# Mixture-of-experts stage of a one-core encoder block: where the filler steps stand between the expert products, and how w1 and w3 lie in a weight block

## The chip, the cores and the metric

The kernel runs on one core of a Trainium2 chip. The metric is the device time of one launch in microseconds (us); less is better. The kernel before took 1903.09 us in the median of three runs (1902.76 to 1908.07).

## The reference, cut to what matters

The block takes 512 tokens of width 1024, mixes them along the sequence (a gated convolution and a state-space branch), and then sends every token through two of 64 experts. Only the second part is touched:

```python
# per expert e, on the tokens that were routed to it
hdn = jax.nn.silu(xblk @ w1[e]) * (xblk @ w3[e])   # w1, w3: 1024 x 512
y   = hdn @ w2[e]                                  # w2: 512 x 1024
h  += g2 * (weight of the token for e) * y         # scattered back to the tokens
```

All weights are float32: 2 MB (2,097,152 bytes) each for w1, w3 and w2 of an expert, 6.29 MB for an expert and 402.7 MB for all 64. Every expert has 64 slots for tokens; what is over that goes to a later round, which is not part of this story.

## The kernel before, in words

**Stages.** The first 800 us or so compute the modulation, the norms, the mixer and the routing. From then on the experts are worked off in 32 pairs (loop in line 1462), the two experts of a pair one behind the other. Four kinds of work run on TensorE (PE) there:

- **W**, in `hidden` (line 1289): the first product. For each of eight slices k of the width, two matmuls with the 64 tokens as stationary operand (64 columns of the array each, `128*64` in the profile) and 512 columns of weights moving: 256 of w1 and the same 256 of w3, one row of the operand `w[k // 4][:, k % 4, :, 256 * j:256 * j + 256]`. One matmul of the program stands as two records in the trace, so an expert has 32 records `ps_w<-wb,xg`.
- **Y**, in `second` (line 1311): the second product, 16 records `ps_y<-wb,ht`, also on 64 columns.
- **g**, a step of `gather` (line 1272): 12 bfloat16 matmuls of 128 columns, `ps_g<-S,hg`, with the full array, which collect 128 channels of the tokens of the next pair. Behind the fourth and the eighth step ScalarE copies four slices of `xg` out of PSUM.
- **c**, a step of `combine` (line 1337): two matmuls `ps_o<-yh,so` and `ps_o<-yl,so` with the full array and 512 columns, which scatter scaled outputs of the last pair to a tile of tokens; VectorE then adds the sum in PSUM to `h` (`h<-h,ps_o`). There are two such sums in PSUM (`po`, line 1225), used in turn, so the third step of a row needs the addition of the first to be over.

`hidden_t` puts two transposes (`ps_ht`) between W and Y. A pair needs eight g and eight c.

**The order on PE** is written out by hand (everything runs in program order on every engine). The table `FILL` (line 1375) has ten places for each of the two experts, divided by commas, and the experts by a semicolon. Places 0 to 7 stand ahead of the matmuls of slice k = 0 to 7, place 8 between W and the transposes, place 9 between the transposes and Y. `FILL0` to `FILL2` are for pairs 0 to 2 and `FILL3` is for the last, so `FILL` holds for the 28 pairs from 3 to 30:

```python
FILL = [v.split(",") for v in ",,,,c,,c,g,gg,gc;c,,c,g,c,,c,,gg,gc".split(";")]
...
for k in range(KD):
    fill(k)
    for j in range(2):
        PE.matmul(ps[64 * j:64 * j + 64], lhsT=xg[:, k, 64 * e:64 * e + 64],
                  rhs=w[k // 4][:, k % 4, :, 256 * j:256 * j + 256], start=(k == 0), stop=(k == KD - 1))
```

**The weights** come through a ring of eight blocks of 16 KB on every partition (`load_upto`, line 741), filled by the queue of SyncE (SP). An expert takes three: slices 0 to 3 of w1 and w3, slices 4 to 7 of both, and w2. At the start of the expert whose first block is b the program has asked for all blocks up to b + 7; a DMA waits on SP until the block that lay in its place has been read for the last time. For the first two blocks of an expert there are two DMAs of 1 MB (line 754), one from w1 and one from w3:

```python
t = t.rearrange("p (k i f) -> p k i f", i=2, k=4)
for k, m in [(0, 2), (2, 2)] if fine else [(0, 4)]:
    for i, n_ in enumerate(("w1", "w3")):
        SP.dma_start(t[:, k:k + m, i], a[n_][e].rearrange("(p k) f -> p k f", k=KD)[:, 4 * part + k:4 * part + k + m])
```

In HBM the four slices of a partition are one piece of 8 KB. In the block the 2 KB rows of w1 and w3 alternate. w2 comes in one DMA of 2 MB (line 765), its pieces 8 KB on both sides. `fine` holds for the early blocks up to 23 and the last expert, whose DMAs are cut in two.

**Between the pairs** (`scale_y`, line 1321) VectorE scales Y, ScalarE rounds it to `yh`, VectorE takes the rest `yl`, GpSimd makes the 0/1 matrix `so`. These feed the c of the next pair.

Of the kernel before, what the change touches and what calls it, by code (L numbers as in the profile page):

```python
# [19 lines left out]
T = 512          # tokens  # L20
D = 1024         # model width
KD = D // P      # k-tiles of the model width; channel d = 8 * p + k
NE = 64          # experts
CAP = 64         # slots of an expert per round
# [39 lines left out]
# columns of the packed per-partition parameters  # L64
# [9 lines left out]
# order in which the 128-column tiles of w_in are used  # L74
# [21 lines left out]
class Meter:  # L96
    """An engine whose instructions' time is added up (us, from their shapes)."""
# [31 lines left out]
def hybrid_block(ctx: ExitStack, tc: tile.TileContext, a, out, dbg=None, stage=9):  # L129
# [11 lines left out]
    # ------------------------------------------------------------ constants  # L141
# [20 lines left out]
    def rstd_start(r, v):  # L162
        """r = 1/sqrt(v + eps) of a [P, 512] array (v may lie in PSUM)."""
        S.activation(r, v, AF.Ln, bias=epsc, scale=1.0)
        S.activation(r, r, AF.Exp, scale=-0.5)

    def rstd_end(r, t, v):
        """A Newton step for it."""
        V.tensor_mul(t, r, r)
        V.scalar_tensor_tensor(t, v, EPS, t, op0=OP.add, op1=OP.mult)  # L170
        V.tensor_scalar(t, t, -0.5, 1.5, op0=OP.mult, op1=OP.add)
        V.tensor_mul(r, r, t)

    def rsqrt_small(r, v, t1, t2, scale=1.0):
        """r = 1/sqrt(scale * v + eps) of a few columns, with a Newton step."""
        V.tensor_scalar(t1, v, scale, EPS, op0=OP.mult, op1=OP.add)
        S.activation(t2, t1, AF.Sqrt)
        V.reciprocal(r, t2)
        V.tensor_mul(t2, r, r)
        V.tensor_mul(t2, t2, t1)  # L180
        V.tensor_scalar(t2, t2, -0.5, 1.5, op0=OP.mult, op1=OP.add)
        V.tensor_mul(r, r, t2)

    # The mixer is emitted in the order in which its engines run it. It goes in slots: one tile of
    # weights each, of about five microseconds of the tensor engine; between the products of two
    # slots stand the small steps of the state-space branch and of the norms, and the vector engine
    # works on the long convolution in what the slots leave.
# [8 lines left out]
    accyf = blky.tile([P, KD * T], F32, name="accy")     # y_ssm, later h  # L196
# [4 lines left out]
    accv = blk.tile([P, KD, T], F32, name="accv")     # conv of the GLU branch  # L201
# [30 lines left out]
    def warm_up(n):  # L232
        """Keeps the tensor engine's clock up where it would wait for others."""
# [4 lines left out]
    # ------------------------------------------------------------ adaLN (shift, scale), norm1, first slots  # L238
    with tc.tile_pool(name="start", bufs=1, side="right") as sp:
# [25 lines left out]
        for k in range(KD):  # L265
            for sec, acc in ((0, acc_sh), (1, acc_sc)):
                w_ = ada_load(k, sec)
                ada_step(acc, w_, k)
                if WK <= k < WKE:                              # keeps the tensor engine's clock up
# [9 lines left out]
        # the sums over the partitions, channels on partitions; more than the one column, for the clock  # L279
# [29 lines left out]
    # ------------------------------------------------------------ buffers of the slots  # L309
# [4 lines left out]
    lsum = wkA.tile([P, T], F32, name="lsum")           # sum over the channels' tiles  # L314
# [3 lines left out]
    causal = wk.tile([P, P], F32, name="causal")       # [s, l]: l >= s  # L318
# [3 lines left out]
    tabs = wk.tile([P, 4, 4, 32], F32, name="tabs")      # [s, table, chunk, head]  # L322
    eend = wk.tile([P, 4, 32], F32, name="eend")         # exp(sum of a chunk), on all partitions
    sdram = dram.tile([2, 32, T], F32, name="sdram")
    deferred = []                                        # work of the scalar engine behind the next slot's weights
    bg = []                                              # work of the vector engine for every slot
# [4 lines left out]
    def taps(n):  # L331
        """Steps of the convolutions in progress, in turns: the steps of one wait for each other."""
# [7 lines left out]
    # dt: softplus, cumulative sums, in steps  # L340
    def dt_tables(ps):
# [44 lines left out]
        # full: the sums over a chunk of 128; loc: over its halves  # L386
# [10 lines left out]
        # what is left of the chunk behind s  # L397
# [21 lines left out]
    def ev_ub(i):  # L419
        def ev(ps):  # L420
            while i > 2 and i - 3 not in done:           # its place
                taps(1)
# [10 lines left out]
    def conv31(i):  # L433
        """The 31 taps of a tile, a tap in a step; then its part of the mean."""
# [11 lines left out]
    def xbc(tl, ps, dst):  # L446
        """A tile of xbc: causal convolution of 4 taps, SiLU."""
# [28 lines left out]
    def ssd(g):  # L476
        """The scan of a group of heads: a stage behind each slot."""
# [12 lines left out]
        # exp(min(sum_l - sum_s, 0)) of a pair of heads, in three steps; C with the decay from the  # L490
        # chunk's start
# [32 lines left out]
        def times_dt(ps, cs):  # L524
            """Tokens on partitions: x * dt, and with the decay to the end of the chunk."""
# [47 lines left out]
        # behind the first slot of z  # L573
# [79 lines left out]
    # ------------------------------------------------------------ slots  # L653
# [73 lines left out]
    # ------------------------------------------------------------ end of the mixer  # L727
    # blocks of 16 KB for the experts' weights: three for an expert, in memory as the mixer leaves it
# [12 lines left out]
    def load_upto(n):  # L741
        while len(wblocks) <= min(n, 3 * NE - 1):
# [7 lines left out]
            if part < 2:  # L750
                t = t.rearrange("p (k i f) -> p k i f", i=2, k=4)
# [17 lines left out]
    B_ = {}                                              # tiles of the end of the mixer  # L769

    def open_end():
        gp.close()
        B_["tk"] = wpools["tk"] = tk = ctx.enter_context(tc.tile_pool(name="tk", bufs=1, side="left", reuse_waits="tile"))
        B_["tcv"] = tk.tile([P, KD, T], F32, name="tcv")           # gated branch
        # the tables of the routing, later a third of the residual stream
# [21 lines left out]
    def ada():  # L797
        """The rest of adaLN: halves of sections, on the scalar engine and GpSimd, two rows in a step."""
# [50 lines left out]
    def layernorm():  # L849
        """LayerNorm and SiLU of the convolution branch."""  # L850
# [49 lines left out]
    def routing_constants():  # L900
# [4 lines left out]
        io(c_("rev", [P, 8]), [[-1, 8]], 8, 0)                      # 8 .. 1  # L905
        tri = c_("tri", [P, P], BF)                                 # [s, t]: s < t
# [4 lines left out]
        io(c_("slot2", [P, 2, CAP]), [[512, 2], [1, CAP]], 0, 0)    # 512 * r + slot  # L911
        io(c_("slotd", [P, 2, CAP]), [[0, 2], [1, CAP]], 0, 0)      # slot, twice
        io(c_("tokp", [P, 4]), [[P, 4]], 1, 1)                      # 1 + 128 * tile + p
        yield

    def router():
        """Router weights times (1 + scale) * norm2_g, and its constant term (on all partitions)."""
# [34 lines left out]
    # the mixer's output projection and the residual; token-major copies: hg with its columns  # L952
    # in the order (k, p), h in the natural order
    def mix(i):
        def mm(w):
            xr = B_["sc"][1 + i % 2]
            SP.dma_start(xr, a["xT"][:, i])
            # the last tile in two halves of the tokens
# [27 lines left out]
    def tokens(i):  # L986
        """Token-major copies of a tile of the residual stream: over its rms (hg), and as it is (h)."""
# [62 lines left out]
    for j in range(2, len(slots)):  # L1050
# [9 lines left out]
        late = j != at["mix"] and posts                  # the first products of the last slots need all before  # L1060
# [20 lines left out]
    pss = pst.tile([P, 4, SQN], F32, name="ps_h", tag="st")  # equal columns, for the clock  # L1081
# [25 lines left out]
    # 1 / rms of the tokens  # L1107
# [21 lines left out]
    # ------------------------------------------------------------ routing  # L1129
# [3 lines left out]
    # Small steps that wait for each other: in two halves of the tokens, in turns  # L1133
# [11 lines left out]
    def first_max(v, oh, m, mi):  # L1145
        """The maximum over the last axis, the one-hot of its first place (oh), 8 - place."""
# [11 lines left out]
    def choice(cs):  # L1158
        """The group, the two experts in it."""
# [19 lines left out]
    # exponentials of the softmax over the groups and of that over the experts of the group  # L1179
# [12 lines left out]
    # positions in the experts' lists  # L1192
# [5 lines left out]
    key = tk.tile([P, 2, 4, 1], F32, name="key")          # 512 * expert + position  # L1198
# [20 lines left out]
    # ------------------------------------------------------------ experts  # L1219
# [12 lines left out]
    tok = par                                             # 1 + token, in the place of the parameters  # L1232
    tok_iota = lambda t: G.iota(t, pattern=[[1, T]], base=1, channel_multiplier=0, allow_small_or_imprecise_dtypes=True)

    def onehot(rel, iota, tag="S", dt=F32):
        """[token, slot]: one of the token's assignments (key - base) has the slot."""
# [12 lines left out]
    # hg split exactly into three parts of bfloat16, the second and the third in its own place  # L1249
# [22 lines left out]
    def gather(s):  # L1272
        """The tokens of a pair of experts, in eight steps of 128 channels."""
# [37 lines left out]
    def second(ht, e, w, yps):  # L1311
        n = 0
        for j in range(2):
            for r2 in range(2):
                for x in range(2):
                    half = x ^ e                          # columns of y on the partitions 64x..
# [18 lines left out]
    sums = {}                                            # h of a tile of tokens, in PSUM  # L1335

    def combine(ys):
        """Adds the scaled outputs of a pair of experts to their tokens, in eight steps."""
# [14 lines left out]
    def to_psum():  # L1353
        """h of the first tiles of tokens to PSUM, where the last pair's outputs are added to it."""
# [14 lines left out]
    # other work of the tensor engine beside the products of the two experts of a pair: steps of the  # L1369
    # next gather (g) and of the last pair's combination (c)  # L1370
# [325 lines left out]
```

## Time and profile before

| | |
|---|---|
| median of three runs | 1903.09 us |
| span of the profiled execution, first to last instruction | 1904.8 us |
| the stage of the 28 pairs with `FILL` (first W of pair 3 to the end of pair 30) | about 916 to 1850 us |
| PE busy over the span | 1808.0 us (95%) |
| DMA, rate of the middle of the expert stage | 377 to 379 GB/s |

The profile is that of one execution. Its span is what the parts of the sum are taken from; it lies 1.7 us above the median of the runs. Matmuls are pipelined and a record's length holds its way through the array, so times of PE work are read from start to start, not from lengths.

### The profile page before, as it was taken

The numbers are of one execution on the slowest core, as the hardware profiler recorded it, in microseconds if no ns is written. First come the engines' busy times: TensorE is split into PE (matmuls) and PEld (weight loads), VectorE is DVE, ScalarE is ACT, GpSimd is POOL, SyncE is SP. The second block draws the span as 40 slices with busy tenths as digits, with TensorE's granted clock in tenths as the row PEclk, the third lists the DMA queues.
The fourth block names the chain that finished last, engine by engine and source line by source line (L and its number), as shares of the span: only waits on it lengthen the run. The fifth ranks groups of instructions, "written<-read, shape, count | busy, mean of one in ns | idle before, by whom it ended". The sixth has DMA issues, their size and how long they took to land.

```text
span 1904.8 us, 25480 instructions
## 1 busy us (share of the span) xinstructions
PE 1808.0 (95%) x10188; PEld 1033.9 (54%) x10188; DVE 1091.8 (57%) x1728; ACT 540.1 (28%) x901; POOL 417.6 (22%) x288
## 2 busy tenths in 40 slices
PE   5999999899999999999999999999999999999996
PEld 2677777677677778753444434444443444444342
DVE  6889999989987675535433434343343434334343
ACT  2443545435343734512111111111111111111112
POOL 3123442524424454202101001010100101010011
PEclk8999999999999989999999999999999999999998
DMA  6252522424244668399999999999999999999971
GB/s 247 71 160 63 158 75 76 145 78 155 68 154 155 210 233 294 125 349 337 332 386 378 378 377 376 379 374 383 380 378 377 376 383 371 382 381 376 378 301 45
DMA packets 192793, 506.91 MB, mean 266 GB/s; under 512 B 10208, under 2 KB 14560, under 8 KB 176544
## 3 DMA queue, kind: packets, MB, share of 16 engines
q1 hardware_dynamic: 192672, 505.25, 73.0%
q8 instruction: 82, 1.34, 0.3%
q14 instruction: 39, 0.32, 0.0%
HBM read 502.98 MB, written 2.23 MB: 265 GB/s over the span
## 4 chain that ended last, share of the span: by engine, by line
PE 77%; DVE 15%; issue 4%; ACT 2%; DMA 1%; POOL 0%; SPq 0%; DVEq 0%; ACTq 0%; POOLq 0%
PE ps_w L124 25%; PE ps_y L124 13%; PE ps_mm L124 11%; PE ps_g L124 10%; PE ps_o L124 8%; DVE accv L124 3%; PE ps_ys L124 3%; DVE w_lo L124 3%; PE ps_cv L124 2%; PE ps_mix L124 2%; DVE ct L124 2%; DVE mE L124 1%; PE ps_ht L124 1%; PE ps_ada L124 1%; DMA w_raw<-in_w_in_dram 1%
## 5 line engine op out<-in xcount | busy, mean ns | idle before, releaser
L124 PE MATMUL ps_w<-wb,xg 128*64 128x512 f32 x2048 | 503.1, 606 | 0.0
L124 DVE TENSOR_TENSOR h<-h,ps_o 128x512 f32<-128x512 f32 x252 | 173.2, 688 | 441.1 <-PE ps_o L124 441.1
L124 PEld LDWEIGHTS ps_w<-wb,xg 128*64 128x64 f32 x2048 | 123.8, 136 | 218.5 <-issue 210.4
L124 PE MATMUL ps_y<-wb,ht 128*64 128x512 f32 x1024 | 233.9, 599 | 2.5 <-DVE ht L124 2.5
L124 PE MATMUL ps_mm<-n1h,w_lo 128*128 128x512 f32 x560 | 224.9, 402 | 11.7 <-DVE w_lo L124 11.7
L1329 POOL TENSOR_SCALAR so<-par,tabA 128x512 fp32r<-128x512 f32 x32 | 49.9, 1561 | 832.6 <-PE ps_o L124 801.9
L124 PE MATMUL ps_mm<-n1h,w_hi 128*128 128x512 f32 x560 | 230.2, 411 | 0.2 <-ACT w_hi L216 0.2
L124 PE MATMUL ps_mm<-n1l,w_hi 128*128 128x512 f32 x560 | 223.4, 399 | 0.0
L124 PEld LDWEIGHTS <-hg 128*128 128x128 bf16 x2784 | 160.4, 98 | 98.0 <-issue 97.4
L124 PE MATMUL ps_g<-S,hg 128*128 128x128 bf16 (+1 forms) x2976 | 211.2, 224 | 0.1
L124 DVE SCALAR_TENSOR_TENSOR accv<-u,par,accv 128x511 f32<-128x511 f32 (+29 forms) x240 | 206.1, 900 | 6.1 <-ACT accv L437 4.2
L1298 ACT ACTIVATE sl<-ps_w 128x256 f32<-128x256 f32 x64 | 24.5, 383 | 644.9 <-PE ps_w L124 644.9
L124 DVE TENSOR_TENSOR w_lo<-w_raw,w_hi 128x1024 fp32r<-128x1024 f32 (+1 forms) x103 | 138.5, 1345 | 83.9 <-ACT w_hi L216 76.3
L216 ACT CAST w_hi<-w_raw 128x1024 fp32r<-128x1024 f32 (+1 forms) x103 | 107.2, 1041 | 265.4 <-PE ps_mm L124 104.6
L124 PEld LDWEIGHTS ps_y<-wb,ht 128*64 128x64 f32 x1024 | 68.0, 137 | 134.5 <-issue 129.7
L1286 ACT ACTIVATE xg<-ps_g,cB,cG 128x128 f32<-128x128 f32 x256 | 96.2, 456 | 144.6 <-PE ps_g L124 144.6
L124 PEld LDWEIGHTS ps_o<-yh,so 128*128 128x128 f32 x252 | 47.2, 187 | 156.3 <-issue 145.2
L124 PEld LDWEIGHTS ps_mm<-n1h,w_lo 128*128 128x128 f32 x560 | 108.2, 193 | 40.4 <-DVE w_lo L124 17.3
L124 PE MATMUL ps_o<-yh,so 128*128 128x512 f32 x252 | 124.5, 494 | 2.0 <-DVE h L124 1.3
L124 DVE TENSOR_TENSOR sl<-sl,ps_w 128x256 f32<-128x256 f32 x64 | 38.9, 608 | 148.7 <-ACT sl L1298 148.7
L124 PEld LDWEIGHTS ps_mm<-n1h,w_hi 128*128 128x128 f32 x560 | 108.4, 194 | 26.0 <-issue 2.7
L124 PEld LDWEIGHTS ps_mm<-n1l,w_hi 128*128 128x128 f32 x560 | 108.4, 194 | 24.2 <-issue 2.1
(325 smaller groups left out, 2221.9 us busy)
## 6 DMA issues: line engine op xcount, KB each, us to landing
wb<-in_w_dram SPq DMA_DIRECT2D x244, 1024.0 KB, 7.7
wb<-in_w_dram SPq DMA_DIRECT2D x57, 2048.0 KB, 9.6
w_raw<-in_w_in_dram SPq DMA_DIRECT2D x72, 512.0 KB, 3.6
wb<-in_w_dram SPq DMA_DIRECT2D x52, 512.0 KB, 7.0
ada_w<-in_w_ada_dram SPq DMA_DIRECT2D x64, 256.0 KB, 3.8
ada_w<-in_w_ada_dram SPq DMA_DIRECT2D x16, 512.0 KB, 9.0
mE<-sdram SPq DMA_DIRECT2D x32, 256.0 KB, 5.9
w_raw<-in_w_ssm_dram SPq DMA_DIRECT2D x16, 512.0 KB, 3.5
```

What stands on the lines that cost most here:

```text
L124: return f(*args, **kw)
L216: S.copy(hi[:, :n], raw[:, :n])
L1286: S.activation(xg[:, q], ps[:, i], AF.Identity, bias=cB2[:, q:q + 1], scale=cG2[:, q:q + 1])
L1298: S.activation(sl, ps[:, 0], AF.Silu)
L1329: G.tensor_scalar(st, tok, tabs2[x][0], None, op0=OP.is_equal)
```

## The change

Two edits.

```diff
-                t = t.rearrange("p (k i f) -> p k i f", i=2, k=4)
+                t = t.rearrange("p (i k f) -> p k i f", i=2, k=4)
...
-    FILL = [v.split(",") for v in ",,,,c,,c,g,gg,gc;c,,c,g,c,,c,,gg,gc".split(";")]
+    FILL = [v.split(",") for v in ",,,,cgcc,,,,gg,gc;,,cgcc,,,,,,gg,gc".split(";")]
```

The rest of the diff takes out comments and moves no line number. By the first edit the four slices of w1 lie behind each other in the first 8 KB of a block and those of w3 in the second 8 KB, so a DMA of line 754 writes 8 KB in one piece (4 KB where it is cut in two), and the two halves of the moving operand of W lie 8 KB apart instead of 2 KB. By the second, the first expert of a pair has filler at places 4, 8 and 9 (before: 4, 6, 7, 8 and 9), the second at 2, 8 and 9 (before: 0, 2, 3, 4, 6, 8 and 9). The number of steps stays at eight c and eight g in a pair; four c instead of three stand in its first expert.

On PE, in the first W of pair 3 (`wb_5350` is the block of slices 4 to 7), the difference of the two programs reads so; the rows of the g's twelve matmuls are cut to one:

```order
 L124 MATMUL ps_o<-yl,so 128x512
-L124 MATMUL ps_w<-wb_5350,xg 64x512 x4
-L124 MATMUL ps_o<-yh,so 128x512
-L124 MATMUL ps_o<-yl,so 128x512
-L124 MATMUL ps_w<-wb_5350,xg 64x512 x2
...
-L124 MATMUL ps_w<-wb_5350,xg 64x512 x2
...
+L124 MATMUL ps_g<-S,hg 128x128
+L124 MATMUL ps_o<-yh,so 128x512
+L124 MATMUL ps_o<-yl,so 128x512
+L124 MATMUL ps_o<-yh,so 128x512
+L124 MATMUL ps_o<-yl,so 128x512
+L124 MATMUL ps_w<-wb_5350,xg 64x512 x8
```

A c, a g and two more c now follow each other, and the eight matmuls of slices 4 to 7 are one row.

On VectorE, between the making of `yl` and the first product's gating (`sl<-sl,ps_w`) of the same pair:

```order
 L124 TENSOR_TENSOR yl<-y,yh 128x512
 L124 TENSOR_TENSOR yl<-sl,yh 128x512
-L124 TENSOR_TENSOR h<-h,ps_o 128x512 x2
-L124 TENSOR_TENSOR sl<-sl,ps_w 128x128x2
-L124 COPY ht<-ps_ht 128x256
-L124 TENSOR_TENSOR h<-h,ps_o 128x512 x5
+L124 TENSOR_TENSOR h<-h,ps_o 128x512 x3
+L124 TENSOR_TENSOR sl<-sl,ps_w 128x128x2
+L124 COPY ht<-ps_ht 128x256
+L124 TENSOR_TENSOR h<-h,ps_o 128x512 x4
```

Three additions to `h` instead of two stand ahead of the first expert's gating.

## The prediction, made before the changed kernel was run

> **What bounds the kernel now.** I read first the span, then the stretches of the expert stage, then who waits for whom in it, and last PE's own timeline of one pair.
>
> ```profile
> core 0: 1904.8 us, clock 0.978
> 1100.00:1200.00 100.00, 100.00 (x638) 42.38 (x636) 38.08 (x76) 15.03 (x36) 9.36 (x6) 1.00 1.01 379
> 1300.00:1400.00 100.00, 100.00 (x638) 42.38 (x636) 38.09 (x76) 15.03 (x36) 9.36 (x6) 1.00 1.01 377
> ```
>
> In the two stretches (columns: length, then busy time of PE, weight loads, VectorE, ScalarE, GpSimd, granted clock, DMA share, GB/s) PE is busy for all of 100 us at the full clock. The DMA share is 1.01 too, so two things could be the bound. The waits tell them apart. Of PE's waits from 860 to 1880 us the first is the longest of five kinds, and none of the five is for a DMA; SP's longest are for matmuls that still read a block:
>
> ```profile
> PE ps_ht L124 <- DVE sl L124: 4.1, 4, 2.2
> ...
> SPq L754 <- PE ps_y L124: 288.5, 54, 5.5
> SPq L754 <- PE ps_w L124: 262.6, 53, 5.5
> ```
>
> So the weights wait for PE and PE waits for nobody. How far ahead they are: the DMA of w2 (line 765) below goes out at 1305.12 into the place that slice block 0 of the running expert leaves; eight blocks on, that is w2 of the expert after next, whose Y begins at 1346.30 (timeline below). That is 41 us, of which a landing takes at most 11.7 (the last row: shortest, median, longest time from issue to landing). The place of a w2 comes free when its Y ends, about 1316.4; the second slice block of the third expert on goes there, and its slices are due 3.5 us after 1349.78, 37 us later. The lead is therefore about 25 us at the least.
>
> ```profile
> 1305.12 0.37 SPq L765 DMA_DIRECT2D wb<-in_w_dram  x1
> DMA to landing us min/median/max: 5.1/8.2/11.7
> ```
>
> Now a pair on PE (start, length, what, how many records):
>
> ```profile
> 1316.42 3.60 PE L124 MATMUL ps_w<-wb,xg 128*64 128x512 f32 x16
> 1319.96 0.49 PE L124 MATMUL ps_o<-yh,so 128*128 128x512 f32 x1
> 1320.29 0.39 PE L124 MATMUL ps_o<-yl,so 128*128 128x512 f32 x1
> 1320.61 1.94 PE L124 MATMUL ps_w<-wb,xg 128*64 128x512 f32 x8
> 1322.47 0.50 PE L124 MATMUL ps_o<-yh,so 128*128 128x512 f32 x1
> 1322.81 0.39 PE L124 MATMUL ps_o<-yl,so 128*128 128x512 f32 x1
> 1323.14 1.08 PE L124 MATMUL ps_w<-wb,xg 128*64 128x512 f32 x4
> 1324.15 0.84 PE L124 MATMUL ps_g<-S,hg 128*128 128x128 bf16 x12
> 1324.92 1.08 PE L124 MATMUL ps_w<-wb,xg 128*64 128x512 f32 x4
> 1325.93 1.51 PE L124 MATMUL ps_g<-S,hg 128*128 128x128 bf16 x24
> 1327.28 0.39 PE L124 MATMUL ps_ht<-ident,sl 128*128 128x128 f32 x2
> 1327.51 0.83 PE L124 MATMUL ps_g<-S,hg 128*128 128x128 bf16 x12
> 1328.15 0.48 PE L124 MATMUL ps_o<-yh,so 128*128 128x512 f32 x1
> 1328.47 0.39 PE L124 MATMUL ps_o<-yl,so 128*128 128x512 f32 x1
> 1328.79 3.65 PE L124 MATMUL ps_y<-wb,ht 128*64 128x512 f32 x16
> 1332.38 0.50 PE L124 MATMUL ps_o<-yh,so 128*128 128x512 f32 x1
> ...
> 1346.30 3.66 PE L124 MATMUL ps_y<-wb,ht 128*64 128x512 f32 x16
> 1349.78 2.31 PE L124 MATMUL ps_w<-wb,xg 128*64 128x512 f32 x9
> ```
>
> From start to start a pair is 1349.78 - 1316.42 = 33.36 us. What matters is that a record costs more at an edge than inside a run. Eight W take 1.86 (1320.61 to 1322.47), four 1.01: 0.214 a record, and 0.15 once for each stretch between two fillers. Sixteen W that follow a Y directly take 3.54 = 16 x 0.214 + 0.11, so 0.11 of the 0.15 is lost on leaving the 64 columns; Y shows the same (3.59 ahead of a c at 1328.79, 3.48 ahead of W at 1346.30).
>
> **The change part by part: the places.** In each of 28 pairs six stretches of 64-column work vanish (two in the first expert, four in the second, the c between Y and W among them): 6 x 0.15 = 0.91 us a pair.
>
> The fillers shorten as well. Alone, a c takes 0.66 from its start to the next W (1319.96 to 1320.61; 1322.47 to 1323.14 is 0.67), a g 0.77 (1324.15 to 1324.92). Eight steps lie so in a pair, six c and two g, 5.52 us together; the other two c and six g stand at places 8 and 9 before and after. What joined steps cost, pair 2 shows, and the tail of the kernel for c behind c:
>
> ```profile
> 898.20 0.84 PE L124 MATMUL ps_g<-S,hg 128*128 128x128 bf16 x12
> 898.85 0.48 PE L124 MATMUL ps_o<-yh,so 128*128 128x512 f32 x1
> 899.17 0.40 PE L124 MATMUL ps_o<-yl,so 128*128 128x512 f32 x1
> 899.49 1.08 PE L124 MATMUL ps_w<-wb,xg 128*64 128x512 f32 x4
> ...
> 1887.67 0.40 PE L124 MATMUL ps_o<-yh,so 128*128 128x512 f32 x1
> 1887.90 0.40 PE L124 MATMUL ps_o<-yl,so 128*128 128x512 f32 x1
> 1888.14 0.39 PE L124 MATMUL ps_o<-yh,so 128*128 128x512 f32 x1
> ```
>
> A g ahead of a c takes 0.65 and the two are 1.29 together, against 0.77 + 0.66 = 1.43 apart. In a run of c the records come 0.235 apart, against 0.33 for the two records of a lone c and 0.33 again from its second to W. So c, g, c, c between two stretches of W: 0.33 (first to second record), 0.235 (second record to g, the value of a run, since this junction occurs nowhere), 0.65 (g to c), 0.32, 0.235, 0.235, and 0.33 back to W: 2.33 us. Two such rows replace 5.52 by 4.66, 0.86 less. The bounds: at best a record of 512 columns takes 0.214 and one of g what 12 more of them add (24 take 1.35 from 1325.93, 12 take 0.77: 0.048 each), 6 x 0.214 + 12 x 0.048 = 1.86 a row and 5.52 - 3.72 = 1.80 less per pair; at worst joining gives nothing. I take 0.86, since all terms but one have their own row.
>
> Together 0.91 + 0.86 = 1.77 us a pair, 33.36 to 31.59, and 28 x 1.77 = 49.6 us. With the bounds it is 25 to 76 us.
>
> The Trainium skill, in TensorEngine Tiling (Array Packing), section Key Properties, says that changing the tiling mode drains the engine. By that alone, with the 0.11 that leaving costs in the rows here, the change would be worth 6 x 0.11 x 28 = 18 us and the time 1885; the trace shows edges on both sides that the rule doesn't mention.
>
> Waits that the rows could bring: the third c of a row needs the sum that the first one's addition frees.
>
> ```profile
> 1318.79 0.69 DVE L124 TENSOR_TENSOR yl<-sl,yh 128x512 fp32r<-128x512 f32 x1
> 1320.72 0.69 DVE L124 TENSOR_TENSOR h<-h,ps_o 128x512 f32<-128x512 f32 x1 [1.24 <-PE ps_o L124]
> ```
>
> The addition starts 0.76 after its c and takes 0.69, so the sum is free 1.45 after the row's start; the third c comes after 0.33 + 0.235 + 0.65 + 0.32 + 0.235 = 1.77. That leaves 0.3 us, and I cost it at nothing. If VectorE were busy then, each 0.1 us beyond would cost 5.6 us in all. The second c now comes 1.2 instead of 2.5 us behind the first; its `yl` is ready at 1319.48, before either. VectorE's other work is queued behind the three additions (the first expert's gating), but the 16 records of W's last four slices, 3.6 us, cover them. The fourth and eighth g stay at place 9, so the copies of `xg` stay where they are. GpSimd's `so` only gets its place earlier.
>
> **The 8 KB pieces.** They touch no engine's instructions but W's operand and the DMAs. How many bytes a piece has shows in two stretches of 3 us, the first (1309 to 1312) nearly all w2 in 8 KB packets, the second (1352 to 1355) w1 and w3 in 2 KB packets:
>
> ```profile
> DMA packets 168, 1.23 MB, mean 411 GB/s; under 512 B 7, under 2 KB 7, under 8 KB 21
> ...
> DMA packets 591, 1.18 MB, mean 393 GB/s; under 512 B 16, under 2 KB 16, under 8 KB 591
> ```
>
> A pair is 12.58 MB. With the packets of before its DMA work is 8.39/0.393 + 4.19/0.411 = 31.5 us, with 8 KB for all 30.6. At a pair of 31.59 us either fits, the first by nothing and the second by 1 us. PE doesn't wait for DMAs now, so the pieces save nothing by themselves: 0 us, but they keep room. W's two halves 8 KB apart: records cost 0.214 with 2 KB between the halves and also in Y with none (3.48/16 = 0.217 with its edge), so I cost that at nothing. The next slower spacing of 512-column records here is 0.235, then 0.33: 2048 records x 0.02 = 43 us or x 0.115 = 236 us as the far bounds.
>
> The sum: the profiled 1904.8 becomes 1855.2. Taken off the median of the runs, 1903.1 - 49.6 = **1853.5 us**.
>
> **The rivals.** (1) *The rows save only the edges of W* because joined steps bring no more, or the third c waits 0.3 us and more: 0.91 x 28 = 25 us, 1878. For it: no c, g, c, c exists in the trace. Against: pair 2's joined g and c.
>
> (2) *The DMA becomes the bound.* If the queues can't give more than the 378 GB/s of now, a pair stays at 33.3 us as soon as the lead of 25 us is used up; of 49.6 us half is left, 1878 again. For it: the DMA share of 1.01. Against: 411 GB/s with long packets, and SP's waits of hundreds of us. The Trainium skill, in DMA: Bandwidth & Descriptors, section Bandwidth, gives about 358 GB/s as the HBM side's limit for such loads, which would speak for this rival. By it a pair would take 12.58/0.358 = 35.1 us, longer than it takes now, so the trace doesn't agree (377 and 379 GB/s over 100 us); the HBM Reference, section Specifications (TRN2), gives about 425 for a core alone, which no run here shows so far.
>
> (3) *Slower.* W reads its two halves 8 KB apart, and a record gets longer. It happens in all 2048 records of W on PE, so it decides from 49.6/2048 = 24 ns a record; at the spacing of a lone c (0.33) it would cost 236 us, 2090. For it: nothing but that this distance is new; against: 0 or 2 KB makes no difference.
>
> (4) *The pieces stay 2 KB in the queue.* Then the packets keep their count and the time is 1853 to 1865, as the lead covers most of what 31.5 us of DMA work in 31.6 leaves open.
>
> **How the numbers follow.** My forecast has 0.82, (1) 0.06, (2) 0.05, (3) 0.04, (4) 0.03. For the forecast itself 0.1 us either way in each of the two rows and 0.02 at each of the six edges is about 9 us, 1844 to 1863; with (4) and part of (1), where the third c waits a little, the range is 1844 to 1867, which leaves out rivals (1) and (2) in full and (3). What a measurement can tell from no change is 0.3%, 5.7 us. All but (3) are faster by more; I give 0.94 for faster, 0.02 for within 0.3% (a little of (3) against the gain) and 0.04 for slower.
>
> **What would show it.** Right: W in stretches of 16, 8 and 24 records, at 3.54 to 3.58, 1.82 and 5.30 us; rows of c, g, c, c at 2.33 us; a pair at 31.6 us; PE still without a wait for a DMA; about 398 GB/s, with a DMA share of 0.97 or so, and the packets of 8 KB. Wrong: PE waiting for `h<-h,ps_o` or for blocks, W records over 0.22 us apart inside a stretch, or a pair that stays over 32 us.

## The result and the profile after

The changed kernel takes 1854.52 us in the median of four runs (1852.01 to 1856.45), the kernel before, run beside it, 1905.51 (1902.76 to 1908.07). The ratio is 0.973 (95% interval 0.972 to 0.975): 2.7% faster, 51 us. The forecast was 1853.5, its range 1844 to 1867.

The span of the profiled execution went from 1904.8 to 1854.7 us. First a stretch of the expert stage (columns as in the prediction), then PE's waits from 860 to 1830 us, and SP's longest:

```profile
1300.00:1400.00 100.00, 100.00 (x674) 46.47 (x673) 39.40 (x78) 15.44 (x37) 9.38 (x6) 1.00 0.99 400
...
PE ps_ht L124 <- DVE sl L124: 4.1, 4, 2.2
...
SPq L754 <- PE ps_y L124: 269.7, 106, 3.9
SPq L754 <- PE ps_w L124: 218.2, 53, 5.5
```

The picture is that of before: PE is busy throughout, its longest kind of wait is the same 4.1 us, none is for a DMA, and SP still waits for blocks to be read. Only the rate went up, from 377 to 400 GB/s in this stretch, as the same bytes pass in less time.

The first expert of a pair on PE, to the W of the second. A record's start is the first column.

```profile
1326.33 3.60 PE L124 MATMUL ps_w<-wb,xg 128*64 128x512 f32 x16
1329.86 0.49 PE L124 MATMUL ps_o<-yh,so 128*128 128x512 f32 x1
1330.19 0.39 PE L124 MATMUL ps_o<-yl,so 128*128 128x512 f32 x1
1330.42 0.84 PE L124 MATMUL ps_g<-S,hg 128*128 128x128 bf16 x12
1331.08 0.48 PE L124 MATMUL ps_o<-yh,so 128*128 128x512 f32 x1
1331.39 0.40 PE L124 MATMUL ps_o<-yl,so 128*128 128x512 f32 x1
1331.63 0.39 PE L124 MATMUL ps_o<-yh,so 128*128 128x512 f32 x1
1331.86 0.40 PE L124 MATMUL ps_o<-yl,so 128*128 128x512 f32 x1
1332.19 3.65 PE L124 MATMUL ps_w<-wb,xg 128*64 128x512 f32 x16
1335.78 1.51 PE L124 MATMUL ps_g<-S,hg 128*128 128x128 bf16 x24
...
1342.12 0.60 PE L124 MATMUL ps_w<-wb,xg 128*64 128x512 f32 x2
```

The row c, g, c, c starts at 1329.86 and W goes on at 1332.19: 2.33 us. Its junctions are 0.33, 0.23, 0.66, 0.31, 0.24, 0.23 and 0.33; the one that no row of before had, from c to g, is 0.23. The second stretch of W takes 3.59, as a stretch of 16 between fillers should. This expert has taken 15.79 us (1326.33 to 1342.12), the one ahead of it, the second of its pair, 15.81 (1310.52, below, to 1326.33). A pair is 31.60.

```profile
1310.52 1.89 PE L124 MATMUL ps_w<-wb,xg 128*64 128x512 f32 x8
1312.34 0.50 PE L124 MATMUL ps_o<-yh,so 128*128 128x512 f32 x1
...
1314.68 5.37 PE L124 MATMUL ps_w<-wb,xg 128*64 128x512 f32 x24
1319.98 1.51 PE L124 MATMUL ps_g<-S,hg 128*128 128x128 bf16 x24
```

In the second expert 8 W take 1.82, the row 2.34, 24 W 5.30. From 33.36 to 31.60 is 1.76 us, times 28 pairs 49.3 of the 50.1 us between the spans.

The packets, from 1000 to 1700 us:

```profile
DMA packets 37536, 278.85 MB, mean 398 GB/s; under 512 B 3536, under 2 KB 3536, under 8 KB 3536
q1 hardware_dynamic: 37489, 278.16, 97.9%
```

All of the weights come in packets of 8 KB now (the 3536 packets that are shorter are all under 512 B), and the share of the DMA engines is 0.98 at 398 GB/s.

### The profile page after: what moved, and what is told of

It reads as the page before. It is cut to its first block, busy times and chain, and to the rows that moved or that the text cites. A ratio compares the mean times of both kernels' runs of the same rounds, so it can differ in the third digit from the quotient of the medians.

```text
span 1854.7 us, 25500 instructions
## 1 busy us (share of the span) xinstructions
PE 1758.9 (95%) x10188; PEld 1048.2 (57%) x10188; DVE 1086.1 (59%) x1728; ACT 540.1 (29%) x901; POOL 417.6 (23%) x288
## 4 chain that ended last, share of the span: by engine, by line
PE 75%; DVE 16%; issue 4%; ACT 2%; DMA 1%; POOL 0%; SPq 0%; DVEq 0%; ACTq 0%; POOLq 0%
PE ps_w L124 24%; PE ps_y L124 13%; PE ps_mm L124 12%; PE ps_g L124 10%; PE ps_o L124 7%; DVE accv L124 4%; DVE w_lo L124 3%; PE ps_cv L124 2%; PE ps_mix L124 2%; PE ps_ys L124 2%; DVE mE L124 2%; DVE ct L124 2%; DVE xs L124 1%; PE ps_ht L124 1%; PE ps_ada L124 1%
## 5 line engine op out<-in xcount | busy, mean ns | idle before, releaser
L124 PE MATMUL ps_w<-wb,xg 128*64 128x512 f32 x2048 | 470.7, 597 | 0.0
L124 DVE TENSOR_TENSOR h<-h,ps_o 128x512 f32<-128x512 f32 x252 | 167.9, 686 | 286.1 <-PE ps_o L124 286.1
L124 PEld LDWEIGHTS ps_w<-wb,xg 128*64 128x64 f32 x2048 | 138.7, 137 | 268.1 <-issue 265.8
L124 PE MATMUL ps_o<-yh,so 128*128 128x512 f32 x252 | 117.1, 465 | 2.0 <-DVE h L124 1.3
L844 POOL TENSOR_TENSOR ada_acc<-ada_acc,ada_w 128x512 f32<-128x512 f32 x56 | 89.9, 1607 | 110.6 <-ACT ada_w L842 108.7
```

The source lines that it names most:

```text
L124: return f(*args, **kw)
L844: G.tensor_add(acc, acc, w)
```

## The experiments

The theory: PE is the bound, and each place at which fillers interrupt the 64-column work has a price of its own; the pieces bring nothing. The main rival: the DMA, with a share of 1.01 before, is the real limit, or comes to be it, so that the 8 KB pieces are needed for the gain.

**Each half of the change alone.** The places with the old layout:

```diff
-                t = t.rearrange("p (i k f) -> p k i f", i=2, k=4)
+                t = t.rearrange("p (k i f) -> p k i f", i=2, k=4)
```

> The new table of places, the old layout with 2 KB pieces. Theory (PE is the bound, the places alone bring the gain): a pair of 31.6 us as in the changed kernel, time 1852 to 1857; the DMA needs 398 GB/s of packets that gave 366 to 393 in single stretches, so its share goes to about 1.05, and what is missing is taken from the lead of 25 us, without a wait of PE. Rival (the 8 KB pieces are needed for the gain): pairs of 32 to 33.3 us once the lead is used up, PE waits for blocks, time 1865 to 1880.

Measured: 1856.65 us (1851.27 to 1858.16), ratio to the kernel before 0.975 (0.973 to 0.977); the changed kernel's interval (0.972 to 0.975) overlaps with it. A stretch, PE's longest kind of wait, the landings of the 1 MB DMAs from 1000 to 1700 us, and VectorE's step at the end of two pairs running:

```profile
1300.00:1400.00 100.00, 100.00 (x675) 46.73 (x674) 38.76 (x77) 16.57 (x40) 9.38 (x6) 1.00 1.03 397
...
PE ps_ht L124 <- DVE sl L124: 4.1, 4, 2.2
...
wb<-in_w_dram SPq DMA_DIRECT2D x176, 1024.0 KB, 13.2
...
1318.11 0.24 DVE L124 TENSOR_SCALAR rel<-key 128x8 f32<-128x8 f32 x1
1349.71 0.24 DVE L124 TENSOR_SCALAR rel<-key 128x8 f32<-128x8 f32 x1
```

A pair is the same 31.60 us. The queue is fuller (share 1.03), and a landing takes 13.2 us instead of 8.3 in the changed kernel; it grows from 9.5 us (920 to 1000 us) to 15.1 (1600 to 1750). That ends inside the lead: PE doesn't wait. So the places alone bring the whole gain that can be measured.

The pieces with the old table:

```diff
-    FILL = [v.split(",") for v in ",,,,cgcc,,,,gg,gc;,,cgcc,,,,,,gg,gc".split(";")]
+    FILL = [v.split(",") for v in ",,,,c,,c,g,gg,gc;c,,c,g,c,,c,,gg,gc".split(";")]
```

> The new layout with 8 KB pieces, the old table of places. Theory: a pair of 33.36 us as before, since PE waited for no DMA; time 1902 to 1908, ratio 1.000; W's records stay 0.214 us apart although their halves lie 8 KB apart; the DMA share falls from 1.01 to about 0.92. Rival (the pieces bring part of the gain): a pair under 33.2 us, time under 1898. Rival (W reads slower): W's records over 0.22 apart, slower than before.

Measured: 1905.30 us in ten runs, ratio 0.9998 (0.9984 to 1.0013). Stretches of W on PE, and a stretch of the stage:

```profile
1315.29 3.60 PE L124 MATMUL ps_w<-wb,xg 128*64 128x512 f32 x16
1318.82 0.50 PE L124 MATMUL ps_o<-yh,so 128*128 128x512 f32 x1
...
1319.49 1.94 PE L124 MATMUL ps_w<-wb,xg 128*64 128x512 f32 x8
1321.35 0.50 PE L124 MATMUL ps_o<-yh,so 128*128 128x512 f32 x1
...
1300.00:1400.00 100.00, 100.00 (x640) 42.31 (x636) 38.16 (x75) 15.02 (x36) 9.37 (x6) 1.00 0.98 380
```

Sixteen W take 3.53 and eight 1.86 with their halves 8 KB apart, as with 2 KB, so the rival that W reads slower is out. The DMA share fell only to 0.98, not to 0.92, at about the same rate (380 GB/s, 377 before); it hardly tells how much room there is, which the runs on the limit below do.

**Half of the places.** The first expert has its row, the second single steps:

```diff
-",,,,cgcc,,,,gg,gc;,,cgcc,,,,,,gg,gc"
+",,,,cgcc,,,,gg,gc;c,,c,g,c,,,,gg,gc"
```

> New layout; the first expert of a pair has its row c, g, c, c, the second has single steps at places 0, 2, 3 and 4 (one fewer than before, since the first expert now takes four c). Theory (a fixed price per place): of the six places three go, 3 x 0.15, and one row of 2.33 and four single steps (3 x 0.665 + 0.77) stand for 5.52: a pair is 33.36 - 0.46 - 0.42 = 32.48 us, time 1853.5 + 28 x 0.89 = 1878, within 3 us. Rival (the gain hangs on something that only the whole change brings, the DMA's room for instance): a pair at 31.6 to 32.0 or at 33.3 us.

Measured: 1879.35 us (1877.49 to 1882.16), ratio 0.987 (0.985 to 0.989).

```profile
1331.53 0.24 DVE L124 TENSOR_SCALAR rel<-key 128x8 f32<-128x8 f32 x1
1364.02 0.23 DVE L124 TENSOR_SCALAR rel<-key 128x8 f32<-128x8 f32 x1
```

From the step on VectorE at the end of one pair to that of the next it is 32.49 us, where 32.48 was expected. In this table the price goes with the number of places and joined steps.

**The order in a row.** c, c, c, g instead of c, g, c, c:

```diff
-",,,,cgcc,,,,gg,gc;,,cgcc,,,,,,gg,gc"
+",,,,cccg,,,,gg,gc;,,cccg,,,,,,gg,gc"
```

> As the changed kernel, but the rows are c, c, c, g. Theory (the g between is what covers the addition to h): the third c would come 0.33 + 3 x 0.235 = 1.04 us after the row's start, its sum is free after 1.45, so PE waits 0.4 in each of 56 rows, and the restart costs up to 0.1 more: a pair of 32.4 to 32.6 us, time 1876 to 1882, and PE's waits name h. Rival (no wait, the order within a row is free): 31.5 to 31.7 us and 1852 to 1857.

Measured: 1886.31 us (1882.19 to 1886.51), ratio 0.990 (0.988 to 0.992); it gives back 32 of the 51 us, a little more than the 22 to 28 expected. A pair takes 32.63 us (32.4 to 32.6 expected), which is 29 us over the 28 pairs; the rest is no more than runs of one kernel differ by. A row on PE, its wait in total, and the two additions that it waits for on VectorE:

```profile
1311.80 0.49 PE L124 MATMUL ps_o<-yh,so 128*128 128x512 f32 x1
...
1312.60 0.40 PE L124 MATMUL ps_o<-yl,so 128*128 128x512 f32 x1
1313.31 0.50 PE L124 MATMUL ps_o<-yh,so 128*128 128x512 f32 x1 [0.31 <-DVE h L124]
...
PE ps_o L124 <- DVE h L124: 17.7, 57, 0.3
...
1312.57 1.28 DVE L124 TENSOR_TENSOR h<-h,ps_o 128x512 f32<-128x512 f32 x2 [1.24 <-PE ps_o L124]
```

The third c starts 0.71 after the record ahead of it instead of 0.235, 1.51 after the row's start; the first addition, begun at 1312.57, ends about 1313.26, just ahead of it. The row itself names 0.31 us of it, from the end of one record to the start of the next; from start to start 0.47 is lost. So the g in the middle of the row covers the addition, as the prediction had it.

**Fewer places still.** Whole stretches of W, and all six steps of the row behind it:

```diff
-",,,,cgcc,,,,gg,gc;,,cgcc,,,,,,gg,gc"
+",,,,,,,,gcgccg,gc;,,,,,,,,gcgccg,gc"
```

> Two places instead of three: each W runs its 32 records in one stretch, and g, c, g, c, c, g stand at place 8 behind it; 8 KB pieces. Theory (a fixed price per place): an expert is W 6.97, the row 0.65 + 0.56 + 0.65 + 0.56 + 0.47 + 0.70, transposes 0.23, g and c 1.29, Y 3.48 = 15.55 us, a pair 31.1, time 1854.5 - 28 x 0.5 = 1840, within 3 us, if 12.58 MB come in 31.1 us (405 GB/s). Rival (the DMA is at its limit): a pair of 31.6 us at the end of the stage, or waits of PE for blocks, time 1848 and more.

Measured: 1839.90 us (1839.37 to 1842.49), ratio 0.966 (0.964 to 0.967): 14.6 us below the changed kernel's median, so faster than both. One expert on PE:

```profile
1305.14 7.04 PE L124 MATMUL ps_w<-wb,xg 128*64 128x512 f32 x32
1312.11 0.84 PE L124 MATMUL ps_g<-S,hg 128*128 128x128 bf16 x12
...
1317.18 3.65 PE L124 MATMUL ps_y<-wb,ht 128*64 128x512 f32 x16
1320.66 0.60 PE L124 MATMUL ps_w<-wb,xg 128*64 128x512 f32 x2
```

An expert takes 15.52 us (15.55 expected), W 6.97 of it in one piece. The same with 2 KB pieces:

> As the last, with the old layout and 2 KB pieces. With 2 KB pieces the run of the places alone moved 396 GB/s at a share of 1.03: 12.58 MB take 31.8 us, 0.7 more than a pair of 31.1. Theory: over 28 pairs 19 us are missing, the lead of 25 us covers them, so 1840 to 1846, with few waits of PE for blocks at the end, landings much later than 13 us. Rival (the lead is shorter than it looks): 1848 to 1860.

Measured: 1840.86 us (1837.75 to 1841.96), ratio 0.966 (0.964 to 0.967), no difference from 8 KB. The queue moves less, however (the first row is of the 8 KB run, the others of the 2 KB run):

```profile
1300.00:1400.00 100.00, 100.00 (x684) 47.57 (x683) 39.25 (x78) 16.53 (x40) 9.37 (x6) 1.00 1.01 408
```

```profile
1300.00:1400.00 100.00, 100.00 (x675) 47.11 (x674) 38.62 (x77) 16.53 (x40) 9.37 (x6) 1.00 1.04 397
...
wb<-in_w_dram SPq DMA_DIRECT2D x178, 1024.0 KB, 16.5
```

A pair of 31.04 us needs 405 GB/s. With 8 KB pieces it gets them, with 2 KB pieces 397, and the landings slip to 16.5 us (8.5 with 8 KB). With 2 KB they grow from 10.1 us (920 to 1000 us) to 17.8 (1600 to 1750): the lead is being eaten, and the stage ends before it is gone.

**The DMA's limit by itself.** In two kernels PE has less to do, so that the queue must show what it can. They leave out parts of the sums: a c does without the matmul of `yl`, a g without those of two of the three parts of `hg`.

```diff
-                hs = [t[:, c, k] for t in parts] or [hg[:, c, k]]
+                hs = [t[:, c, k] for t in parts[:1]] or [hg[:, c, k]]
...
-                PE.matmul(ps, lhsT=st[:, c * P:(c + 1) * P], rhs=yh, start=c not in sums, stop=False)
-                PE.matmul(ps, lhsT=st[:, c * P:(c + 1) * P], rhs=yl, start=False, stop=True)
+                PE.matmul(ps, lhsT=st[:, c * P:(c + 1) * P], rhs=yh, start=c not in sums, stop=True)
```

> The changed kernel with less for PE to do, so that the DMA is the bound: a step of c leaves out the matmul of yl, and a step of g those of the second and third part of hg from pair 3 on (the sums leave out these parts). PE alone would need 31.6 - 8 x 8 x 0.056 - 8 x 0.235 = 26.1 us a pair. 8 KB pieces. Expected: the last pairs take what the DMA needs, 30.6 us at 411 GB/s (30 to 31), and PE waits for blocks.

> As the last, with 2 KB pieces. Expected: the last pairs take 31.7 us (397 GB/s, what the run of the places alone moved), 1.1 us more than with 8 KB; if the pieces make no difference to the queue, the same as with 8 KB.

Measured, one run each: 1776.94 us with 8 KB, 1828.34 with 2 KB. A stretch of the first, then one of the second with PE's longest kind of wait from 1300 to 1700 us and VectorE's step at the end of two pairs:

```profile
1300.00:1400.00 100.00, 94.28 (x485) 35.21 (x486) 44.52 (x92) 17.46 (x42) 12.49 (x8) 1.00 1.01 420
```

```profile
1300.00:1400.00 100.00, 86.89 (x439) 32.97 (x437) 39.31 (x78) 15.03 (x36) 9.37 (x6) 1.00 1.04 398
PE ps_w L124 <- DMA wb<-in_w_dram: 25.9, 23, 2.3
...
1421.61 0.23 DVE L124 TENSOR_SCALAR rel<-key 128x8 f32<-128x8 f32 x1
1453.19 0.23 DVE L124 TENSOR_SCALAR rel<-key 128x8 f32<-128x8 f32 x1
```

Here the pieces count: 420 GB/s against 398 (397 over other stretches of the stage). In microseconds a pair needs 12.58/0.420 = 30.0 with 8 KB and 12.58/0.397 = 31.7 with 2 KB. The 31.58 us between the last two rows agree with that. PE's own time was missed: the first pairs of both run at 28.9 us and not 26.1, and PE is no longer busy throughout (94.28). It waits for VectorE now: from 1300 to 1700 us of the 8 KB kernel, 15.2 us for the gating ahead of the transposes and 6.5 for the additions to `h`, about 1.6 of the 2.8 us a pair that were missed, so the thinner fillers no longer cover these chains.

The step on VectorE, followed through the stage, also shows when the lead ends. In the 2 KB kernel eight pairs go at 28.9, one at 29.3, and those behind at 31.5 to 32.9. Over the eight, 8 x (31.7 - 28.9) = 22 us were missing, 27 with pair 3 (29.7) and the pair of 29.3. In the 8 KB kernel 21 pairs go at 28.9 and the last five at 29.7 to 30.3; 21 x (30.0 - 28.9) = 23 us. So the lead is some 23 to 27 us by this count.

**One place.** All eight steps behind W, none between the transposes and Y:

```diff
-",,,,cgcc,,,,gg,gc;,,cgcc,,,,,,gg,gc"
+",,,,,,,,gcgccggc,;,,,,,,,,gcgccggc,"
```

> One place instead of two: all eight steps of an expert stand behind W (g, c, g, c, c, g, g, c), none between the transposes and Y. Theory of a fixed price per place alone: the edges of one more place go, about 0.1 to 0.2 us an expert, a pair of 30.7 to 30.9 and a time of 1830 to 1837. Rival (the place between transposes and Y covers the copy of the transposes on VectorE): from the transposes to Y PE takes 0.96 us where nothing stands between, as in pairs 1 and 2 and in the last, instead of 0.22 + 0.64 + 0.64 = 1.51 with g and c, which in the row cost 0.65 + 0.24 = 0.9; an expert is then 0.3 us longer, a pair 31.7, time 1857, and PE waits for ht.

Measured: 1893.01 us (1891.53 to 1896.65), ratio 0.993 (0.991 to 0.995). The direction was the rival's, the size was not: it is 53 us above two places, and an expert takes 16.5 us. PE's rows and wait, then VectorE's:

```profile
1321.25 0.48 PE L124 MATMUL ps_o<-yh,so 128*128 128x512 f32 x1
1321.57 0.39 PE L124 MATMUL ps_o<-yl,so 128*128 128x512 f32 x1
1321.80 0.38 PE L124 MATMUL ps_ht<-ident,sl 128*128 128x128 f32 x2
1323.08 0.65 PE L124 MATMUL ps_y<-wb,ht 128*64 128x512 f32 x2 [0.90 <-DVE ht L124]
...
1322.00 0.69 DVE L124 TENSOR_TENSOR h<-h,ps_o 128x512 f32<-128x512 f32 x1 [1.06 <-PE ps_o L124]
1322.61 0.42 DVE L124 COPY ht<-ps_ht 128x256 f32<-128x256 f32 x1
```

From the transposes to Y it is 1.28 us, of which 0.22 are the transposes: the copy of `ht` has nothing over it, and the last c's addition stands ahead of it on VectorE. I had reckoned with 0.96, and with 0.24 for another c in the row, which cost 0.55 (1321.25 to 1321.80). The two misses are 0.63 us an expert, 35 of the 36 us by which the time lies above the rival's 1857.

## Why the prediction was right

- **PE is the bound, not the DMA.** Right, and shown by each half alone. The queue of before, two thirds of whose bytes come in 2 KB pieces, was put at 31.5 us a pair (399 GB/s) and needs 31.7 (397), a little more than a pair of 31.6 takes: the places alone lived on the lead by that much. With 8 KB pieces it was put at 411 GB/s and gave 420, so the room is 1.6 us a pair (31.6 against 30.0), not 1.
- **The price of a place.** 0.91 + 0.86 = 1.77 us a pair were forecast, 1.76 measured; the row of 2.33 was 2.33 and 2.34, c to g 0.23 where 0.235 was chosen. The half change came out at 32.49 against 32.48, the version with two places at 31.04 against 31.1. What the price of an edge is made of, no run here separates. That the time itself was met within 1 us is in part luck: the runs of one kernel lie up to 8 us apart (1899.67 to 1907.84 with the pieces alone), and the median of before that the forecast was taken off, 1903.1, was 1905.5 beside the changed kernel. The 1.76 us a pair is what the sum can be held to.
- **The wait of the third c**, costed at nothing because of 0.3 us of margin: right, since the changed kernel has no such wait; with 0.4 us too little instead (c, c, c, g) it came, and cost 32 us.
- **The 8 KB pieces at nothing.** Right for the time: 0.9998 alone, and 1854.5 against 1856.7 with the places. They do change the queue (landings of 8.3 instead of 13.2 us), only behind a lead that hides it. From 31.7 us a pair downwards 2 KB pieces live on that lead; 28 pairs of 31.04 end inside it.
- **The drain rule.** The Trainium skill (TensorEngine Tiling (Array Packing), section Key Properties) says that changing the tiling mode drains the engine. The prediction read it as a price on leaving the 64 columns alone, 18 us, and said that the rule doesn't mention the edge on the other side. The section names neither a price nor a direction, and a filler between two stretches of W changes the tiling twice, so the runs speak against this reading and not against the rule. Of the 49 us by the sum, 18 are for leaving the 64 columns, 7 for entering them again, and 24 for fillers that are shorter in a row than alone.
- **The DMA limit.** DMA: Bandwidth & Descriptors of the Trainium skill, section Bandwidth, gives about 358 GB/s as the limit of the HBM side; the runs moved 420 with 8 KB pieces. The same section says that this is each core's share while both cores of an HBM domain stream, and lists 425 for one alone, so its 358 is not the figure for this case. The HBM Reference of the Trainium skill, section Specifications (TRN2), has about 425 for a core alone too, and the measurement sides with that.
- **Smaller misses.** The lead was put at 25 us at the least, and the two counts above give 23 to 27; PE alone in the thin kernels was put at 26.1 us a pair and took 28.9; the DMA share with 8 KB pieces was to fall to 0.97 in the changed kernel and is 0.98, but with the old table 0.98 too, where 0.92 was expected.

## What to carry to other kernels

Where one engine is busy without a gap, read the time from start to start and look for what an interruption costs: the price of a place and of a lone filler, times their number, was the whole gain here, and it could be added up beforehand to 0.01 us a pair. Join fillers as far as something else doesn't need them as cover; each position hides a certain chain (here the addition to `h`, the gating, the copy of `ht`), and taking the last cover away cost 53 us (1893.0 against 1839.9), where the edges that it saved were put at 0.1 to 0.2 us an expert, 6 to 11 us in all. A DMA share of 1.0 didn't say here that the queue was the bound: it stood at 1.01 in the kernel before and at 1.03 with the places alone, and PE waited for no DMA in either. Whether somebody waits for a landing decides, and a kernel with less compute shows the limit itself.

## What the runs showed of the hardware that was not expected

- The queue tops out at 397 GB/s here where two thirds of the bytes come in 2 KB pieces and the rest in 8 KB, and at 420 with 8 KB for all.
- In pair 1, whose PE waits 2.2 us for the gating, the granted clock between 870 and 890 us was 1.00 in the execution of before and 0.83 in that of the changed kernel. The sixteen records of Y behind that wait took 3.48 us from their start to the next W in the first and 6.18 in the second:

```profile
870.00:890.00 20.00, 17.04 (x70) 5.18 (x68) 10.37 (x17) 4.37 (x9) 7.94 (x6) 1.00 0.90 320
...
876.13 3.66 PE L124 MATMUL ps_y<-wb,ht 128*64 128x512 f32 x16 [0.52 <-DVE ht L124]
```

```profile
870.00:890.00 20.00, 17.36 (x60) 5.40 (x60) 7.88 (x13) 2.48 (x5) 5.68 (x4) 0.83 0.81 288
...
872.87 6.34 PE L124 MATMUL ps_y<-wb,ht 128*64 128x512 f32 x16 [0.52 <-DVE ht L124]
```

It was 0.83 with the pieces alone and 1.00 with the places alone, but also 0.83 with two places and 2 KB pieces and 1.00 with half of the places and 8 KB, so it goes with neither edit. Leaving the thin kernels aside, pair 1 takes 53.4 us in the four executions with 1.00 and 56.4 in the five with 0.83, by the same step on VectorE as above. So 3 us of a profiled span can hang on this alone. Between the spans of before and after they cancel by chance: the changed kernel's execution came to that step ahead of pair 0 2.9 us earlier (795.49 against 798.34). Why the clock falls in some executions stays open.
